# Raw output weights in the down-weight pool's five buffers, kept open through the output projection's first half

## The chip, the cores and the metric

The kernel runs on one NeuronCore of a Trainium2 chip. The metric is device time in microseconds (us) of one execution; the kernel before is shown by the median of three runs. TensorE (PE in the profile, PEld for its weight loads), VectorE (DVE), ScalarE (ACT) and GpSimd (POOL) compute, each with its own instruction stream in a fixed order; every DMA of this kernel is issued from SyncE's queue (SP), also in a fixed order, and runs on the core's 16 DMA engines.

## The reference

The program is one hybrid decoder layer on 1040 tokens (16 meta tokens and 1024 inputs) of width 1024, all in float32. Two head groups run in parallel on the same normalised input: four differential-attention heads and four HGRN2 heads (a gated linear recurrence in chunks of 16 tokens). Their outputs, 512 + 512 columns, are joined and multiplied by the output weights `w_out` (1024 x 1024); the result is normalised, added to the stream, and a gated FFN with a width-3 convolution follows.

```python
a = rmsnorm(h, ln_mix_pre[l])
dq, dk, dv, hq, hf, hi, hg = jnp.split(a @ w_in[l], SPLITS, axis=-1)
y_diff = diff_attention(dq, dk, dv, ...)          # 4 heads
y_hgrn = hgrn2(hq, hf, hi, hg, ...)               # 4 heads, recurrence over chunks
mix = jnp.concatenate([y_diff, y_hgrn], axis=-1) @ w_out[l]
h = h + rmsnorm(mix, ln_mix_post[l])
a = rmsnorm(h, ln_ffn_pre[l])
y = conv_ffn(a, w_ffn_up[l], ffn_conv_w[l], ffn_conv_b[l], w_ffn_down[l])
h = h + rmsnorm(y, ln_ffn_post[l])
```

The change concerns the product with `w_out`.

## The kernel before

Float32 products are made from three matmuls of rounded pieces: each operand is split into a high part (a cast by ACT) and a low part (raw minus high, by DVE or POOL), and high x high, high x low and low x high are summed in PSUM. So every weight tile goes through three steps: a DMA brings the raw 128 x 512 tile (256 KB), ACT casts the high part, and DVE or POOL subtracts for the low part.

The raw tiles pass through pools with a set number of buffers. A tile's DMA waits until the last reader of the buffer's former tile is done. The pool `wp` has three such raw buffers (tag `wr`). Another pool, `wsp` ("wdsums"), has five buffers of the same size (tag `wd`); it is used while the heads are computed, by `down_sums`: it loads quarters of the FFN's down weights (`wd11`, `wd12`, `wd21`, `wd22`), DVE subtracts them from each other, and the differences are written to the DRAM scratch `tsc`. Pools are stacked from the left or from the right end of the on-chip memory, and a pool that is closed gives its place to those opened after it. Before, `wsp` lay on the left, opened after the activations' pool and before the attention heads' pool `ap_`, and was closed with both when the last head's projections had been issued (line 923).

The output projection comes in two halves of 512 columns. `out_first` is the first half. It is issued interleaved with the last HGRN head (`hgrn_head`): its matmuls fill PE between that head's steps. Per block of 128 tokens (in the order 2, 3, 4, 5, 6, 7, 8, 1, then the meta tokens) it multiplies seven of the eight weight tiles k = 0 to 6 (the eighth belongs to the HGRN head that is not yet finished), in two parts, k = 0 to 3 and k = 4 to 6. The weights of this half are `wor0_k` (raw), `woh0_k` and `wol0_k` (high and low; for k = 0 and 1 they are called `wh`, `wl`). While it runs, the weights of the second half (`wor1_k`) are loaded and split, two or one per block. The tokens' own operand is split too: `mix_split` makes `mm`i`_0` (k = 0 to 3) and `mm`i`_4` (k = 4 to 6) of block i, with a cast on ACT and a subtraction on DVE, and writes them to the DRAM scratch `msc` by DMA for the second half, which loads them as `mp`.

The recurrence of the HGRN head runs in doubling steps on DVE and PE: DVE scales `mix` and `kr` (the keys), PE multiplies them into `pl`, DVE masks the result into `a` and `am`, and after the last step PE transposes `kr` into `pk` (line 518).

PE's order is written out by hand: the program order, set by `interleave`. On ACT, DVE, POOL and SP a scheduler orders instructions when the program is built, by its own costs and by the order of the code; `tc.issue_after` holds an instruction's place back behind another one. Most helpers on ACT and DVE have line 54.

Of the kernel before, what the change touches and what calls it, by code (L numbers as in the profile page):

```python
# [9 lines left out]
F32 = mybir.dt.float32  # L10
# [7 lines left out]
P = 128  # L18
# [4 lines left out]
KD = D // P  # L23
# [64 lines left out]
def layer_kernel(ctx: ExitStack, tc: tile.TileContext, x, meta, table, lbl, gpre, gpost, win,  # L88
# [6 lines left out]
    def pool(name, bufs, side="left", space=None):  # L95
        kw = {"side": side} if space is None else {"space": space}
        cm = tc.tile_pool(name=name, bufs=bufs, reuse_waits="tile", **kw)
        return cm, cm.__enter__()

    def line_up(where, n):  # L100
        where.tile([P, n], F32, tag=f"lineup{len(lined)}", name=f"lineup{len(lined)}", bufs=1)
        lined.append(n)
# [3 lines left out]
    def close(*cms):  # L106
        for cm in cms:
            cm.__exit__(None, None, None)
# [7 lines left out]
    w_cm, wp = pool("weights", 1, "right")  # L116
# [29 lines left out]
    def ps_in(name):  # L146
        return pp.tile([P, 512], F32, tag="ip", name=name)
# [4 lines left out]
    def ps_s(name):  # L152
        return pp.tile([P, 2, 512], F32, tag="S", name=name)

    def split(hi, lo, raw, eng=None):
        A.copy(hi, raw)
        (eng or G).tensor_tensor(lo, raw, hi.bitcast(F32), op=ALU.subtract)
# [18 lines left out]
    def mix(ks, t0, t1):  # L176
        g = 0 if t1 <= start(3) else 1 if t1 <= start(6) else 2
        base = start(GROUPS[g][0])
        return mixes[g][:, ks, t0 - base:t1 - base]

    at_cm, atp = pool("at", 1)
# [6 lines left out]
        base = start(GROUPS[g][0])  # L188
        return acts[l][g][:, ks, t0 - base:t1 - base]

    ws_cm, wsp = pool("wdsums", 5)
    wsp.tile([P, 32], F32, tag="lineup_ws", name="lineup_ws", bufs=1)

    last_load = []

    def down_sums():
        def load(k):
            with tc.issue_after(last_load[-1].ins):
                for nm, kk, half in (("11", k, 0), ("12", k, 1), ("22", k + NF // 2, 1), ("21", k + NF // 2, 0)):
                    b[nm] = wsp.tile([P, 512], F32, tag="wd", name=f"wd{nm}_{k}")  # L200
                    SY.dma_start(b[nm], wdown[P * kk: P * (kk + 1), 512 * half: 512 * (half + 1)])
            b["t3"] = wsp.tile([P, 512], F32, tag="wd", name=f"wd3_{k}")

        b = {}
        load(0)
        yield
        yield
        for k in range(NF // 2):
            for j, d, p_, q_ in ((2, "t3", "22", "12"), (0, "12", "12", "11"), (1, "22", "22", "12"), (3, "21", "21", "22")):
                with tc.issue_after(V.last.ins):  # L210
                    V.tensor_tensor(b[d], b[p_], b[q_], op=ALU.subtract)
                with tc.issue_after(last_load[-1].ins):
                    SY.dma_start(tsc[j][P * k: P * (k + 1)], b[d])
                yield
            if k + 1 < NF // 2:
                load(k + 1)
                yield
                yield
# [4 lines left out]

    wd_sums = down_sums()
    at_p_cm, ap_ = pool("attn", 1)
    z_cm, zp = pool("pre", 2, "right")

    def load_m(m, name, where=None, bufs=4):
# [143 lines left out]
    def carried():  # L372
        tails = list(carry)
        carry.clear()
        return tails
# [502 lines left out]
    for c in range(2):  # L878
        raw = wp.tile([P, 512], F32, tag="wr", name=f"wr3_{c}", bufs=3)
# [25 lines left out]
    h_cm, hp = pool("hgrn", 1, "right")  # L905
# [14 lines left out]

    assert next(wd_sums, wd_sums) is wd_sums
    line_up(hp, 24)
    close(at_p_cm, ws_cm, at_cm)
    y_cm, yp = pool("y0", 1)
    y0 = yp.tile([P, NBLK, 512], F32, tag="y0", name="y0")
    m0 = yp.tile([P, KD, 36], F32R, tag="m0", name="m0")
# [10 lines left out]
    ma_cm, map_ = pool("mixsplit", 4)  # L937
    w0_cm, w0p = pool("wo0", 1)
    line_up(w0p, 16)

    FIRST = (2, 3, 4, 5, 6, 7, 8, 1)
    kept = kpp.tile([P, 2, KD, P], F32R, tag="kept", name="kept")

    def load_wr(n, k):
        raw = wp.tile([P, 512], F32, tag="wr", name=f"wor{n}_{k}", bufs=3)
        last_load.append(SY.dma_start(raw, wout[P * k: P * (k + 1), 512 * n: 512 * (n + 1)]))
        return n, k, raw

    def load_wo(n, k, raw):
        if k < 2:  # L950
            where, tag, bufs = wp, ("wh", "wl"), 4
        elif n == 0 and k < KD - 1:
            where, tag, bufs = w0p, ("woh", "wol"), KD - 3
        else:
            where, tag, bufs = w1p, ("woh", "wol"), KD - 1
        hi, lo = (where.tile([P, 512], F32R, tag=t, name=f"{t}{n}_{k}", bufs=bufs) for t in tag)
        split(hi, lo, raw, V if n or k else G)
        return hi, lo

    def tok(i):  # L960
        return (2, 14) if i == 0 else (P, start(i))

    def mix_split(i, k0, k1):
        r, t0 = tok(i)
        src = mix(slice(k0, k1), t0, t0 + r)
        if i < 2:
            hi, lo = (kept[:, 0, k0:k1], kept[:, 1, k0:k1]) if i else (m0[:, k0:k1, 0:2], m0[:, k0:k1, 32:34])
        elif k1 - k0 == 1:
            m = mlp.tile([P, 2, 1, P], F32R, tag="m1", name=f"mm{i}_{k0}", bufs=7)
            hi, lo = m[:, 0], m[:, 1]  # L970
        else:
            m = map_.tile([P, 2, k1 - k0, P], F32R, tag="mm", name=f"mm{i}_{k0}")
            hi, lo = m[:, 0], m[:, 1]
        A.copy(hi, src)
        V.tensor_tensor(lo, src, hi.bitcast(F32), op=ALU.subtract)
        if i > 1 and k1 < KD:
            for c in range(k0 // 2, (k1 + 1) // 2):
                ka, kb = max(k0, 2 * c), min(k1, 2 * c + 2)
                SY.dma_start(msc[i, c][:, :, P * (ka - 2 * c):P * (kb - 2 * c)],
                             m[:, :, ka - k0:kb - k0].bitcast(F32).rearrange("p l k t -> p l (k t)"))  # L980
        return hi, lo, k0, k1, r

    def out_part(sp_, py, wo, first, last, ks=None):
        mh, ml, k0, k1, r = sp_
        for k in ks or range(k0, k1):
            hi, lo = wo[k]
            j = k - k0
            T.matmul(py[:r], mh[:, j, :r], hi, start=(first and j == 0), stop=False)
            yield 216
            T.matmul(py[:r], mh[:, j, :r], lo, start=False, stop=False)  # L990
            yield 216
            T.matmul(py[:r], ml[:, j, :r], hi, start=False, stop=(last and k == k1 - 1))
            yield 216
# [4 lines left out]
                T.matmul(py[:34], m0[:, k, :34], wo[k][l], start=(k == 0 and l == 0), stop=(k == last and l == 1))  # L998
                yield 216

    sps = [mix_split(i, 0, 4) for i in FIRST[:2]]
    mix_split(0, 0, 7)
    wo0 = [load_wo(*load_wr(0, k)) for k in range(KD)]
    wo = []

    pre_last = {}
# [19 lines left out]
    def mix_load(i, c):  # L1026
        m = mlp.tile([P, 2, 2, P], F32R, tag="mp", name=f"mp{i}_{c}", bufs=4)
        n = 1 if c == 3 else 2
        last_load.append(SY.dma_start(m[:, :, :n].bitcast(F32).rearrange("p l k t -> p l (k t)"), msc[i, c][:, :, : n * P]))
        return m[:, 0], m[:, 1], 2 * c, 2 * c + n, P  # L1030
# [3 lines left out]
    def out_first():  # L1034
        pys = [ps_s(f"py0_{i}")[:, 0] for i in FIRST[:2]]
        for ks in ((0, 1), (2, 3)):
            for j in range(2):
                yield from out_part(sps[j], pys[j], wo0, ks[0] == 0, False, ks)
        sqs = [mix_split(i, 4, 7) for i in FIRST[:2]]
        for j in range(2):  # L1040
            yield from out_part(sqs[j], pys[j], wo0, False, True)
            if j == 0:
                sp_ = mix_split(FIRST[2], 0, 4)
            A.copy(y0[:, FIRST[j]], pys[j])
        nxt = [load_wr(1, k) for k in (0, 1)]
        for n, i in enumerate(FIRST[2:]):
            for w in nxt:
                with tc.issue_after(V.last.ins):
                    wo.append(load_wo(*w))
            nxt = [load_wr(1, k) for k in ((2, 3), (4,), (5,), (6,), (7,), ())[n]]  # L1050
            if n == 3:
                ahead.extend(mix_load(2, c) for c in range(4))
            py = ps_in(f"py0_{i}")
            sq_ = mix_split(i, 4, 7)
            yield from out_part(sp_, py, wo0, True, False)
            if i != FIRST[-1]:
                sp_ = mix_split(FIRST[n + 3], 0, 4)
            yield from out_part(sq_, py, wo0, False, True)
            A.copy(y0[:, i], py)
        py = ps_in("py0_0")  # L1060
        yield from out_meta(py, wo0, 0, 7, 6)
        A.copy(y0[:2, 0], py[32:34])
        V.tensor_tensor(y0[:2, 0], y0[:2, 0], py[:2], op=ALU.add)
        while 0 not in finished:
            yield None
        for p in range(3):
            pre_last[p] = mix_split(p, 7, 8)
        for p in range(3):
            yield from out_last(p)

    interleave(out_first(), [hgrn_head(t_h, finished)] + carried(), FO, 4200)
    close(w0_cm, ma_cm, h_cm)

    sw_cm, swp = pool("sums", 1, "right")
    e_cm, ep = pool("early", 1, "right")
# [166 lines left out]
    for n, i in enumerate(order):  # L1242
# [9 lines left out]
        nxt = []  # L1252
# [507 lines left out]
```

## Time and profile before

| what | value |
|---|---|
| time, median of 3 runs | 1304.05 us (1303.45 to 1305.43) |
| the profiled execution, time | 1303.76 us |
| its span, first to last instruction | 1302.0 us |
| PE busy | 1270.9 us, 98% of the span |
| DVE, ACT, POOL busy | 913.7, 691.4, 408.7 us |
| granted TensorE clock | 0.999 |
| DMA | 153.07 MB, 118 GB/s on average |

The profiled execution took 1303.76 us, of which its span is 1302.0 us; the rest lies around it. The page's slices of the span show PE at nine tenths or more in all but the first and the last slice, at a full granted clock. The output projection's first half runs from about 518 us to 582 us of the span. In the rows of the timeline the columns are start and duration in us, engine, line, operation, result <- operands, size, count, and in brackets the idle time before it with what ended it.

### The profile page before, as it was taken

The page shows a single profiled execution, that of the slowest core. Times are in us where ns is not written, and L with a number is a line of the kernel's source. Part 1 is how long each engine was busy: PE and PEld are TensorE (multiplying, and loading weights), DVE is VectorE, ACT ScalarE, POOL GpSimd, SP SyncE. Part 2 cuts the span into 40 slices and gives each one's busy share as a digit, 9 for nine tenths or more (in the row PEclk, how much of TensorE's full clock was granted, in tenths as well). Part 3 has the DMA queues.
Part 4 walks back from the last instruction along what each step waited for, and adds up shares of the span by engine and source line. Part 5 has one row for each costly group of instructions (what it writes and reads, how often), then busy time and mean ns, then how long its engine had stood idle before and what let it go on. Part 6 is the DMA issues. An engine that isn't in the chain of part 4 may idle for free.

```text
span 1302.0 us, 26327 instructions
## 1 busy us (share of the span) xinstructions
PE 1270.9 (98%) x10236; PEld 1181.6 (91%) x10236; DVE 913.7 (70%) x1577; ACT 691.4 (53%) x1672; POOL 408.7 (31%) x322
## 2 busy tenths in 40 slices
PE   7999999999999999999999999999999999999997
PEld 6899999999998999777899999999999998888886
DVE  7575656575757565746888787787787787697587
ACT  7465356545653566446665454455455454454454
POOL 3211212021212120013155666766766740010020
PEclk9999999999999999999999999999999999999999
DMA  6221323122322211836711322222222236965363
GB/s 221 93 90 62 100 90 105 54 99 98 98 78 91 77 38 44 268 106 206 260 58 66 106 93 79 74 97 75 74 98 74 74 106 218 333 203 172 94 210 122
DMA packets 84371, 153.07 MB, mean 118 GB/s; under 512 B 9571, under 2 KB 19843, under 8 KB 84246
## 3 DMA queue, kind: packets, MB, share of 16 engines
q1 hardware_dynamic: 84246, 151.39, 35.2%
q8 instruction: 80, 1.31, 0.4%
q14 instruction: 45, 0.37, 0.1%
HBM read 112.69 MB, written 38.67 MB: 116 GB/s over the span
## 4 chain that ended last, share of the span: by engine, by line
PE 87%; DVE 6%; ACT 3%; DMA 2%; issue 1%; SPq 0%; DVEq 0%; ACTq 0%
PE pd L1571 5%; PE pd L1572 5%; PE pd L1570 5%; PE pb L1371 4%; PE pb L1372 4%; PE pb L1373 4%; PE pa L722 3%; PE pa L1372 3%; PE pa L1371 3%; PE pa L1373 3%; PE pc L1371 3%; PE pc L1373 3%; PE pc L1372 3%; PE pq L1350 2%; PE pq L1348 2%; PE pq L1349 2%
## 5 line engine op out<-in xcount | busy, mean ns | idle before, releaser
L1371 PE MATMUL pb<-t,uh 128*128 128x258 f32 (+1 forms) x456 | 127.4, 279 | 0.4 <-DVE u L54 0.4
L1372 PE MATMUL pb<-t,uh 128*128 128x258 f32 (+1 forms) x456 | 127.3, 279 | 0.0
L1373 PE MATMUL pb<-t,ul 128*128 128x258 f32 (+1 forms) x456 | 127.2, 279 | 0.0
L1571 PE MATMUL pd<-wl,gh 128*128 128x512 f32 (+1 forms) x314 | 120.8, 385 | 0.4 <-DVE wl L54 0.3
L1572 PE MATMUL pd<-wh,gl 128*128 128x512 f32 (+1 forms) x314 | 120.8, 385 | 0.0
L1570 PE MATMUL pd<-wh,gh 128*128 128x512 f32 (+1 forms) x314 | 120.7, 384 | 0.0
L54 DVE SCALAR_TENSOR_TENSOR c<-uu,cwt,c 128x512 f32<-128x512 f32 x88 | 94.7, 1077 | 22.3 <-ACT c L54 21.5
L1320 POOL TENSOR_TENSOR c<-c,c 128x512 f32<-128x512 f32 x44 | 64.4, 1463 | 127.2 <-ACT c L54 113.7
L54 DVE SCALAR_TENSOR_TENSOR c<-ug,cwt,c 128x512 f32<-128x512 f32 x88 | 84.0, 955 | 6.6 <-ACT c L54 5.9
L1371 PEld LDWEIGHTS pb<-t,uh 128*128 128x128 f32 x456 | 85.9, 188 | 0.8 <-DVE u L54 0.6
L1372 PEld LDWEIGHTS pb<-t,uh 128*128 128x128 f32 x456 | 85.9, 188 | 0.0
L1373 PEld LDWEIGHTS pb<-t,ul 128*128 128x128 f32 x456 | 85.8, 188 | 0.0
L1372 PE MATMUL pa<-t,uh 128*128 128x256 f32 (+1 forms) x304 | 85.3, 281 | 0.0
L1373 PE MATMUL pa<-t,ul 128*128 128x256 f32 (+1 forms) x304 | 85.2, 280 | 0.0
L1371 PE MATMUL pa<-t,uh 128*128 128x256 f32 (+1 forms) x304 | 85.2, 280 | 0.0
L1373 PE MATMUL pc<-t,ul 128*128 128x256 f32 x304 | 83.9, 276 | 0.0
L1371 PE MATMUL pc<-t,uh 128*128 128x256 f32 x304 | 83.9, 276 | 0.0
L1372 PE MATMUL pc<-t,uh 128*128 128x256 f32 x304 | 83.9, 276 | 0.0
L1571 PEld LDWEIGHTS pd<-wl,gh 128*128 128x128 f32 x314 | 59.0, 188 | 13.7 <-DVE wl L54 1.5
L1572 PEld LDWEIGHTS pd<-wh,gl 128*128 128x128 f32 x314 | 59.0, 188 | 12.0
L1570 PEld LDWEIGHTS pd<-wh,gh 128*128 128x128 f32 x314 | 59.0, 188 | 11.9
L54 ACT ACTIVATE c<-ug,cbt,cwt 128x512 f32<-128x512 f32 x44 | 35.9, 816 | 44.1 <-issue 26.2
(411 smaller groups left out, 4285.7 us busy)
## 6 DMA issues: line engine op xcount, KB each, us to landing
ra<-in_wup_dram SPq DMA_DIRECT2D x76, 256.0 KB, 2.7
wd<-in_wdown_dram SPq DMA_DIRECT2D x44, 256.0 KB, 3.3
tsc<-wd SPq DMA_DIRECT2D x44, 256.0 KB, 2.1
gsc<-c SPq DMA_DIRECT2D x44, 256.0 KB, 2.0
wi<-tsc SPq DMA_DIRECT2D x44, 256.0 KB, 3.0
gi<-gsc SPq DMA_DIRECT2D x33, 256.0 KB, 3.8
wi<-in_wdown_dram SPq DMA_DIRECT2D x33, 256.0 KB, 3.3
msc<-mm SPq DMA_DIRECT2D x21, 256.0 KB, 4.6
```

The lines of the kernel that those rows point to most:

```text
L54: ins = call(*args, **kw)
L722: T.matmul(po[:, :P], w_, vn[:, j], start=(j == 0), stop=(j == i))
L1320: G.tensor_tensor(cg, cg, cu, op=ALU.mult)
L1348: T.matmul(pt, hi[:, s], th[:, k], start=(kh + k == 0), stop=False)
L1349: T.matmul(pt, hi[:, s], tl[:, k], start=False, stop=False)
L1350: T.matmul(pt, lo[:, s], th[:, k], start=False, stop=(kh == 1 and k == 3))
L1371: T.matmul(pt, hi[:, s], th[:, k], start=(first and k == 0), stop=False, skip_group_check=True)
L1372: T.matmul(pt, hi[:, s], tl[:, k], start=False, stop=False, skip_group_check=True)
L1373: T.matmul(pt, lo[:, s], th[:, k], start=False, stop=(k == 3), skip_group_check=True)
L1570: T.matmul(py, gh[:, s], wh, start=(k == 0 and pr not in (3, 7)), stop=False, skip_group_check=True)
L1571: T.matmul(py, gh[:, s], wl, start=False, stop=False, skip_group_check=True)
L1572: T.matmul(py, gl[:, s], wh, start=False, stop=(k == NH - 1), skip_group_check=True)
```

## The change

The pool `wsp` moves from the left to the right end of the memory, so that it lies next to `wp`, and it is no longer closed before the output projection but after its first half, together with the HGRN pool. `load_wr` now puts only the first three raw tiles of the first half (k = 0, 1, 2) into `wp`'s three buffers; all others go into the five buffers of `wsp`, which `down_sums` has done with by then. All eight loads of the first half are written ahead of the first `mix_split`s, and of the second half's loads four instead of two are written ahead of the block loop, which then keeps more loads ahead of the splits. Small pads (`line_up`) are moved with the pools. The pools of the attention and HGRN heads thereby lie 10,240 bytes lower in each partition; what is opened after the first half lies where it did.

```diff
-    ws_cm, wsp = pool("wdsums", 5)
-    wsp.tile([P, 32], F32, tag="lineup_ws", name="lineup_ws", bufs=1)
+    ws_cm, wsp = pool("wdsums", 5, "right")
...
     wd_sums = down_sums()
     at_p_cm, ap_ = pool("attn", 1)
+    line_up(ap_, 32)
...
-    close(at_p_cm, ws_cm, at_cm)
+    close(at_p_cm, at_cm)
...
     def load_wr(n, k):
-        raw = wp.tile([P, 512], F32, tag="wr", name=f"wor{n}_{k}", bufs=3)
+        raw = (wp.tile([P, 512], F32, tag="wr", name=f"wor{n}_{k}", bufs=3) if n == 0 and k < 3
+               else wsp.tile([P, 512], F32, tag="wd", name=f"wor{n}_{k}"))
         last_load.append(SY.dma_start(raw, wout[P * k: P * (k + 1), 512 * n: 512 * (n + 1)]))
         return n, k, raw
...
-    sps = [mix_split(i, 0, 4) for i in FIRST[:2]]
+    wors = [load_wr(0, k) for k in range(KD)]
+    with tc.issue_after(last_load[-1].ins):
+        sps = [mix_split(i, 0, 4) for i in FIRST[:2]]
     mix_split(0, 0, 7)
-    wo0 = [load_wo(*load_wr(0, k)) for k in range(KD)]
+    wo0 = [load_wo(*w) for w in wors]
...
-        nxt = [load_wr(1, k) for k in (0, 1)]
+        nxt = [load_wr(1, k) for k in range(4)]
         for n, i in enumerate(FIRST[2:]):
-            for w in nxt:
+            for w in [nxt.pop(0) for _ in range((2, 2, 1, 1, 1, 1)[n])]:
                 with tc.issue_after(V.last.ins):
                     wo.append(load_wo(*w))
-            nxt = [load_wr(1, k) for k in ((2, 3), (4,), (5,), (6,), (7,), ())[n]]
+            nxt += [load_wr(1, k) for k in ((4,), (5,), (6,), (7,), (), ())[n]]
...
-    close(w0_cm, ma_cm, h_cm)
+    close(w0_cm, ma_cm, h_cm, ws_cm)
```

PE's and POOL's orders stay as they were. On SP, before the output projection, where the last loads of the input weights (`wr_hg3`) and the last writes of the differences (`tsc`) stand, the rows were, before:

```order
L213 DMA tsc_93<-wd3_10_5284 128x512
L163 DMA wr_hi3_1_5698<-in_win_dram 128x512
L163 DMA wr_hg3_0_5887<-in_win_dram 128x512
L213 DMA tsc_93<-wd12_10_5278 128x512
L213 DMA tsc_93<-wd22_10_5280 128x512
L213 DMA tsc_93<-wd21_10_5282 128x512
L163 DMA wr_hg3_1_5893<-in_win_dram 128x512
L946 DMA wor0_0_6343<-in_wout_dram 128x512
L946 DMA wor0_1_6349<-in_wout_dram 128x512
L946 DMA wor0_2_6355<-in_wout_dram 128x512
L946 DMA wor0_3_6361<-in_wout_dram 128x512
L946 DMA wor0_4_6367<-in_wout_dram 128x512
```

and are now:

```order
L212 DMA tsc_93<-wd3_10_5284 128x512
L947 DMA wor0_3_6336<-in_wout_dram 128x512
L163 DMA wr_hi3_1_5698<-in_win_dram 128x512
L163 DMA wr_hg3_0_5887<-in_win_dram 128x512
L212 DMA tsc_93<-wd12_10_5278 128x512
L947 DMA wor0_4_6338<-in_wout_dram 128x512
L212 DMA tsc_93<-wd22_10_5280 128x512
L947 DMA wor0_5_6340<-in_wout_dram 128x512
L212 DMA tsc_93<-wd21_10_5282 128x512
L947 DMA wor0_6_6342<-in_wout_dram 128x512
L947 DMA wor0_7_6344<-in_wout_dram 128x512
L163 DMA wr_hg3_1_5893<-in_win_dram 128x512
```

The five loads that take over buffers of the differences stand each behind the write that frees its buffer, and ahead of the last input weight; the three that stay in `wp` follow after it. The loads `wor0_5` to `wor0_7` stood much later before, behind the first writes to `msc`.

On ACT, at the start of the first half, the rows were, before (`sg` is the HGRN head's gate, `m0` and `kept` the splits of the meta tokens and of block 1):

```order
L54 CAST mm2_4_6461<-mix0_99 128x384
L54 ACTIVATE sg3_2_6292<-pi_hg3_2_6250 128x384
L54 CAST m0_6306<-mix0_99 128x7x2
L54 CAST mm3_4_6466<-mix1_100 128x384
L54 CAST kept_6330<-mix0_99 128x512
L54 ACTIVATE sg3_2_6292<-sg3_2_6292,one_80 128x384
L54 CAST kept_6330<-mix0_99 128x384
L54 ACTIVATE sg3_2_6292<-sg3_2_6292 128x384
L54 CAST mm4_0_6485<-mix1_100 128x512
L54 CAST woh0_5_6375<-wor0_5_6373 128x512
L54 CAST woh0_6_6381<-wor0_6_6379 128x512
L54 CAST woh0_7_6387<-wor0_7_6385 128x512
```

and are now:

```order
L54 CAST woh0_5_6378<-wor0_5_6340 128x512
L54 ACTIVATE sg3_2_6292<-pi_hg3_2_6250 128x384
L54 CAST m0_6305<-mix0_99 128x7x2
L54 CAST woh0_6_6382<-wor0_6_6342 128x512
L54 CAST woh0_7_6386<-wor0_7_6344 128x512
L54 ACTIVATE sg3_2_6292<-sg3_2_6292,one_80 128x384
L54 CAST mm2_4_6460<-mix0_99 128x384
L54 ACTIVATE sg3_2_6292<-sg3_2_6292 128x384
L54 CAST mm3_4_6465<-mix1_100 128x384
L54 CAST kept_6329<-mix0_99 128x512
L54 CAST mm4_0_6484<-mix1_100 128x512
L54 CAST wh1_0_6548<-wor1_0_6540 128x512
```

The casts of `woh0_5` to `woh0_7` come ahead of the tokens' splits, and the place behind `mm4_0` is taken by `wh1_0`, the first weight of the second half.

On ACT, near the end of the first half (`am` are copies for the HGRN head's masked products), the rows were, before:

```order
L54 CAST mm7_0_6847<-mix2_101 128x512
L54 CAST woh1_5_6862<-wor1_5_6804 128x512
L54 COPY y0_6305<-py0_5_6685 128x512
L54 CAST mm7_4_6877<-mix2_101 128x384
L54 CAST woh1_6_6929<-wor1_6_6866 128x512
L54 COPY am_736<-a323_6415 32x8x32 x4
L54 CAST mm8_0_6908<-mix2_101 128x512
L54 CAST woh1_7_7010<-wor1_7_6933 128x512
L54 COPY y0_6305<-py0_6_6806 128x512
L54 CAST mm8_4_6936<-mix2_101 128x384
```

and are now:

```order
L54 CAST mm7_0_6848<-mix2_101 128x512
L54 CAST woh1_7_7009<-wor1_7_6867 128x512
L54 COPY y0_6304<-py0_5_6686 128x512
L54 CAST mm7_4_6878<-mix2_101 128x384
L54 COPY am_736<-a323_6414 32x8x32 x4
L54 CAST mm8_0_6909<-mix2_101 128x512
L54 COPY y0_6304<-py0_6_6807 128x512
L54 CAST mm8_4_6935<-mix2_101 128x384
```

`woh1_7`, the last weight, moves up by one block, to where `woh1_5` stood, and no weight's cast stands between `mm7_4` and `mm8_4` any more.

## The prediction

> **What bounds the kernel now.** I read the engines' shares first, then the busy time by stretch, then what PE waited for, and then the timeline of PE, ACT, DVE and SP at each wait. First the page's engine rows, then the stretches of the span (per engine: us busy, instructions in brackets; then PE clock, DMA share, GB/s):
>
> ```profile
> PE 1270.9 (98%) x10236; PEld 1181.6 (91%) x10236; DVE 913.7 (70%) x1577; ACT 691.4 (53%) x1672; POOL 408.7 (31%) x322
> ...
> 525.00:532.00 7.00, 5.35 (x85) 3.41 (x84) 5.12 (x12) 4.47 (x8) 0.00 (x0) 1.00 0.96 328
> 532.00:555.00 23.00, 23.00 (x386) 17.88 (x386) 18.27 (x48) 9.59 (x19) 2.34 (x5) 1.00 0.82 250
> 555.00:560.00 5.00, 3.18 (x16) 2.33 (x15) 2.38 (x5) 1.99 (x4) 0.00 (x0) 1.00 0.34 115
> ```
>
> PE is the bound: a change is worth what it opens or closes in PE's stream. The first half of the output projection has two holes, 7.00 - 5.35 = 1.65 us of idle time before 532 and 5.00 - 3.18 = 1.82 us before 560; between them PE is full. What each waited for, from PE's and ACT's timelines:
>
> ```profile
> 524.88 0.39 PE L990 MATMUL py<-wol,mm 128*128 128x512 f32 x1
> 525.11 0.39 PE L992 MATMUL py<-woh,mm 128*128 128x512 f32 x1
> 526.64 0.51 PE L988 MATMUL py<-woh,mm 128*128 128x512 f32 x1 [1.15 <-ACT woh L54]
> ...
> 528.67 0.49 PE L580 MATMUL ssa<-ident,ona 128*128 128x128 f32 x3
> ...
> 530.36 0.69 PE L462 MATMUL pl<-mix,kr 128*32 128x16 f32 x62 [0.28 <-DVE am L54]
> ...
> 534.00 0.70 PE L462 MATMUL pl<-mix,kr 128*32 128x16 f32 x62
> ...
> 555.94 0.40 PE L992 MATMUL py<-woh,mm 128*128 128x512 f32 x1
> 558.16 0.55 PE L518 MATMUL pk<-ident,kr 128*128 128x128 f32 x3 [1.82 <-DVE kr L54]
> ```
>
> ```profile
> 522.55 0.62 ACT L54 CAST mm<-mix 128x512 fp32r<-128x512 f32 x1 [1.17 <-PE py L992]
> 525.97 1.93 ACT L54 CAST woh<-wor 128x512 fp32r<-128x512 f32 x3 [2.80 <-DMA wor<-in_wout_dram]
> ...
> 545.41 0.62 ACT L54 CAST woh<-wor 128x512 fp32r<-128x512 f32 x1 [1.86 <-DMA wor<-in_wout_dram]
> ...
> 555.13 0.62 ACT L54 CAST woh<-wor 128x512 fp32r<-128x512 f32 x1 [3.44 <-DMA wor<-in_wout_dram]
> 556.13 0.51 ACT L54 CAST mm<-mix 128x384 fp32r<-128x384 f32 x1
> ```
>
> Both begin with a raw output weight that has not landed. At 525.97 ACT has stood 2.80 us before `woh0_5`, which PE needs next. At 555.13 it has stood 3.44 us before `woh1_7`, which nobody needs yet; but the cast of `mm8_4` is queued behind it, and behind that, on DVE, `kr`:
>
> ```profile
> 526.62 0.69 DVE L54 TENSOR_TENSOR wol<-wor,woh 128x512 fp32r<-128x512 f32 x1 [2.73 <-ACT woh L54]
> ...
> 530.94 0.36 DVE L54 TENSOR_TENSOR mix<-mix,f 128x192 f32<-128x192 f32 x1 [0.26 <-PE pl L462]
> 531.21 0.69 DVE L54 TENSOR_TENSOR mm<-mix,mm 128x512 fp32r<-128x512 f32 x1
> 531.82 0.69 DVE L54 TENSOR_TENSOR kr<-kr,f 128x520 f32<-128x520 f32 x1
> 532.43 0.56 DVE L54 TENSOR_TENSOR mix<-mix,f 128x136 f32<-128x136 f32 x2
> ...
> 552.93 0.28 DVE L54 TENSOR_TENSOR mix<-mix,tt 128x128 f32<-128x128 f32 x1
> 556.67 0.56 DVE L54 TENSOR_TENSOR mm<-mix,mm 128x384 fp32r<-128x384 f32 x1 [3.46 <-ACT mm L54]
> ...
> 557.42 0.69 DVE L54 TENSOR_TENSOR kr<-kr,tt 128x512 f32<-128x512 f32 x1
> ```
>
> Why the weights are late stands in SP's queue and in the time from issue to landing of the eleven `wor` loads after 515 us:
>
> ```profile
> 446.68 8.18 SPq L213 DMA_DIRECT2D tsc<-wd  x3
> 460.04 0.33 SPq L163 DMA_DIRECT2D wr_hg<-in_win_dram  x1
> 461.29 40.06 SPq L946 DMA_DIRECT2D wor<-in_wout_dram  x5
> ...
> 519.81 1.53 SPq L946 DMA_DIRECT2D wor<-in_wout_dram  x3
> ...
> 548.30 0.56 SPq L946 DMA_DIRECT2D wor<-in_wout_dram  x1
> ...
> 566.36 12.37 SPq L1231 DMA_DIRECT2D rap<-in_wup_dram  x4
> DMA to landing us min/median/max: 2.9/4.7/6.8
> ```
>
> With three buffers only five loads are out before 502; `wor0_5` is issued at 519.81, when an earlier split has freed a buffer, and lands 6.2 us later, at 525.97.
>
> **The first hole.** The five extra loads now go out behind the writes of the differences (446.68 to 454.86), and `wor0_0` to `wor0_2` take the three old buffers. All eight land by about 482, since the last old buffer is freed by the split of the second `wr_hg`, whose cast comes at 476.2 (row below). ACT then casts `woh0_5` to `woh0_7` before 521, with no wait. Without it PE runs on from 525.11: nine matmuls of three weight steps at 0.23 us (524.88 to 525.11), plus some 0.3 us for the HGRN head's three `ssa` transposes between them (528.67), bring the next `pl` to 525.11 + 10 x 0.23 + 0.3 = 527.75 instead of 530.36. That is 2.6 us; the idle time of 1.65 is its lower bound, as the restarts at 0.50 us are also paid.
>
> A part is lost to ACT's new order. `wh1_0` now stands behind `mm4_0`, and its load is issued where `wor0_5` was and should land as late, at 526. So ACT still stands from 523.2 to 526, takes three weight casts (1.93 us) and only then `mm4_4`; PE needs that one late, but DVE's subtraction for it stands before the doubling step. By the rows that is 528.4 for the cast's end, then on DVE about 0.5 each for `mm4_4` and `kept`, as their shape is that of 556.67, and 0.3, 0.6, 0.6 and 0.5 for the four rows from 530.94 on, by the distance of their starts: 531.4 to 531.8. PE would be at its second `pl` at 527.75 + (534.00 - 530.36) = 531.4. I take 0.35 us off, bounds 0 and 1.0 (one load a us later). First term: 2.25 us, bounds 1.3 and 2.6.
>
> **The second hole.** `wor1_7` went out at 548.30, when the split of `wor1_4` had freed a buffer. With five buffers it gets that of `wor1_2`, split two blocks earlier, and goes out about 538, in SP's order behind two `mp` loads. Its cast moves to the place where `woh1_5` stood, and no weight stands between `mm7_4` and `mm8_4`. It should land at 543, by the median of 4.7 us, when ACT arrives at 541 (545.41 - 1.86 in the row of `woh1_5`, less the first term); `woh1_5` cost 1.86 us there and PE stayed full (23.00 of 23.00). Then `mm8_4` is cast as soon as its block is done, DVE goes from 552.93 straight to `mm`, `mix` and `kr` (some 1.6 us by the rows from 556.67 to the end of `kr`: done by 554.7), and PE finds `kr` ready at 555.94 + 0.23 = 556.17 instead of 558.16. Second term: 2.0 us. Its lower bound is 0, if `wor1_7` takes 6.8 us and stalls DVE's chain at the new place by as much.
>
> **Moved and added at no cost.** The casts and subtractions are as many as before (16 weights, 0.62 us on ACT and 0.69 on DVE by the rows of 555.13 and 526.62), only in another order. SP gains waits: `wor0_3`, `wor0_5`, `wor0_6` and `wor0_7` wait until the difference in their buffer has been written out, and behind them stands `wr_hg3_1`, issued at 460.04. These writes land within 2.1 us:
>
> ```profile
> tsc<-wd SPq DMA_DIRECT2D x4, 256.0 KB, 2.0
> ...
> L54 ACT CAST wh_hg<-wr_hg x2: 620/620/621, 472.9 to 476.2; 128x512 fp32r<-128x512 f32 x2
> ```
>
> That ends near 457, before the buffer of `wr_hg3_1` is free, and its cast comes at 476.2, so 13 us of cover lie behind that. Should the writes take longer than this, ACT and then PE's gate projection would wait for the rest. After 582 the orders are the old ones and follow PE. The sum is 2.25 + 2.0 = 4.25 us, less 0.1 for the small things: the span of 1302.0 becomes 1297.9, the profiled run's 1303.76 becomes 1299.6, and the median of the runs, 0.29 above that run, 1299.9 us.
>
> The Trainium skill, "SBUF — State Buffer", section "The DMA setup-cost knee", gives a transfer some 2 us fixed plus its bytes at 436 GB/s: an estimate of 2.6 us for 256 KB by that page. By it `wor0_5` would have landed at 522.4, before ACT was free at 523.2, and the first term would be nothing. The trace does not agree where it counts: 6.2 us here, a median of 4.7, with the DMA engines at 0.96 between 525 and 532.
>
> **Rivals.** (a) One hole stays or comes back elsewhere. Either `wor1_7` lands late at its new place, or `wh1_0` and its followers hold ACT longer in the first stretch. For it speaks that the loads out after 519 are as many and the engines at 0.96; against it that the loads come earlier than their use by a block. It leaves one term: 1304.05 - 2.1 = 1302.0. (b) The change doesn't do what it says: the stand merely moves from `woh0_5` to `wh1_0` and on to what PE needs. For it: the same landing time, 526. Against it: behind `wh1_0` PE first needs `mm4_4`, five us later. Time: 1303.5 to 1304.5. (c) Slower, through SP after the first half: `rap0_11`, the first FFN weight, was issued at 566.36 into the place of `kr`. With the HGRN pool 10 KB lower its place is that of `on`, the normalised HGRN output, which PE reads last in the `ss` transposes at 576.87; all SP rows behind it, the loads of `gpo` and `xh` among them, wait too, and on ACT its cast stands at 580.72. Its rows, the landing of the four `rap` loads, and a later wait of PE:
>
> ```profile
> 576.87 0.55 PE L580 MATMUL ss<-ident,on 128*128 128x128 f32 x3
> ...
> 580.72 1.73 ACT L54 CAST uh<-rap 128x512 fp32r<-128x512 f32 x3
> ...
> 588.87 0.60 ACT L54 ACTIVATE at<-py 128x512 f32<-128x512 f32 x1 [3.21 <-PE py L992]
> ...
> DMA to landing us min/median/max: 2.6/2.8/4.0
> ...
> PE py L988 <- DMA mp<-msc: 0.8, 1, 0.8
> ```
>
> Before, the second `rap` load waited for that same read, so the queue only gets one issue (0.4 us) later, and a landing in 2.6 to 4.0 us puts the cast at most 1 us late, against 3.21 us that ACT idles next. It decides from 3.2 us on; to make the kernel 0.2% slower it would have to be 4.1 + 2.6 + 3.2, some 10 us late: 1307. On this queue the Trainium skill, "DMA: Bandwidth & Descriptors", section "Anatomy of one DMA", says that a semaphore wait happens on the issuing sequencer and not in the DMA engines; by it, (c) has a queue behind it, as I have taken it.
>
> **Numbers.** 0.2% is 2.6 us, about what a measurement of this kernel can tell from no change. Forecast (both holes close): 0.70, 1298.7 to 1301.3. (a) 0.15 and (b) 0.10, both within 0.2% for the most part. (c) and other losses 0.05. Faster 0.71, same 0.24, slower 0.05. The range runs from 1298.6 (2.6 + 2.0 and the 0.8 us that PE waits for `mp` later, should that wait go too) to 1302.6, past (a), with (b) and (c) left out.
>
> **What would show it.** In the profile of the changed kernel: ACT's `woh0_5` cast before 520 with no wait; no PE wait for `woh` or `wol` near 525; the `pk` transposes within 0.3 us of the matmul before them; `wor1_7` issued before 541. A PE wait on `pl` for `mix` or `am` between 529 and 536 would be the lost part of the first term. I am wrong if PE waits there for more than a us, if ACT stands at `woh1_7` beyond 545, or if PE's waits after 600 grow beyond the 0.8 us for `mp`.

## The result, and the profile after

The changed kernel takes 1299.62 us, median of 8 runs (1299.01 to 1300.77); the kernel before 1303.43 us, median of 8 (1301.70 to 1305.43). The medians differ by 3.8 us. The ratio on record is 0.9974, with a 95% interval of 0.9964 to 0.9985, so 0.26% or 3.4 us faster (2.0 to 4.7). A second series of 11 runs beside other kernels gave 1300.33 us against 1303.57, ratio 0.9979 (0.9971 to 0.9988). The profiled execution after took 1299.51 us, its span is 1297.7 us, so 4.3 us less than the profiled span before, as the working had it (4.1).

The page's engine rows and the stretches of the span after, with the same columns as before:

```profile
PE 1269.4 (98%) x10236; PEld 1180.8 (91%) x10236; DVE 913.6 (70%) x1577; ACT 691.9 (53%) x1672; POOL 410.3 (32%) x322
...
525.00:532.00 7.00, 7.00 (x158) 5.42 (x156) 4.78 (x13) 6.09 (x12) 0.00 (x0) 1.00 1.03 351
532.00:555.00 23.00, 23.00 (x337) 18.04 (x330) 18.70 (x48) 8.71 (x18) 2.49 (x5) 1.00 0.70 229
555.00:560.00 5.00, 5.00 (x30) 4.32 (x29) 0.99 (x3) 1.07 (x2) 0.00 (x0) 1.00 0.01 2
```

PE is full in all three stretches: the 1.65 and the 1.82 us of idle time are gone. PE's timeline after:

```profile
525.00 0.39 PE L993 MATMUL py<-woh,mm 128*128 128x512 f32 x1
525.22 0.39 PE L989 MATMUL py<-woh,mm 128*128 128x512 f32 x1
...
527.73 0.71 PE L462 MATMUL pl<-mix,kr 128*32 128x16 f32 x62
...
531.36 0.74 PE L462 MATMUL pl<-mix,kr 128*32 128x16 f32 x62
...
553.31 0.39 PE L993 MATMUL py<-woh,mm 128*128 128x512 f32 x1
553.55 0.49 PE L518 MATMUL pk<-ident,kr 128*128 128x128 f32 x3
```

The matmul behind the one at 525.00 starts 0.22 us later where it stood 1.15 us before; `pl` comes at 527.73 (before: 530.36), and the `pk` transposes at 553.55 (before: 558.16), 0.24 us behind the matmul ahead of them. On ACT:

```profile
516.45 2.17 ACT L54 CAST woh<-wor 128x512 fp32r<-128x512 f32 x4
...
525.44 0.62 ACT L54 CAST wh<-wor 128x512 fp32r<-128x512 f32 x1 [2.37 <-DMA wor<-in_wout_dram]
...
544.45 0.62 ACT L54 CAST woh<-wor 128x512 fp32r<-128x512 f32 x1 [3.48 <-DMA wor<-in_wout_dram]
```

`woh0_5` is the last of the four casts from 516.45 on, with no wait. ACT still stands 2.37 us, now before `wh1_0`, and 3.48 us before `woh1_7`, but PE did not wait for what is queued behind them in this execution. After 560 us the longest of PE's waits are these:

```profile
PE py L989 <- DMA mp<-msc: 0.7, 1, 0.7
PE pz L989 <- DVE y L54: 0.7, 1, 0.7
PE pb L1374 <- DVE u L54: 0.6, 1, 0.6
```

### The profile page after: what moved, and what is told of

The parts are those of the page before. It is cut to its first block, busy times and chain, and to the rows that moved or that the text cites. A ratio compares the mean times of both kernels' runs of the same rounds, so it can differ in the third digit from the quotient of the medians.

```text
span 1297.7 us, 26321 instructions
## 1 busy us (share of the span) xinstructions
PE 1269.4 (98%) x10236; PEld 1180.8 (91%) x10236; DVE 913.6 (70%) x1577; ACT 691.9 (53%) x1672; POOL 410.3 (32%) x322
## 4 chain that ended last, share of the span: by engine, by line
PE 87%; DVE 7%; ACT 2%; DMA 2%; issue 1%; SPq 0%; POOL 0%; DVEq 0%; ACTq 0%; POOLq 0%
PE pd L1574 5%; PE pd L1575 5%; PE pd L1573 4%; PE pb L1374 4%; PE pb L1375 4%; PE pb L1376 4%; PE pa L722 3%; PE pa L1375 3%; PE pa L1374 3%; PE pa L1376 3%; PE pc L1376 3%; PE pc L1374 3%; PE pc L1375 3%; PE pq L1353 2%; PE pq L1351 2%; PE py L989 2%
## 5 line engine op out<-in xcount | busy, mean ns | idle before, releaser
L1198 POOL TENSOR_TENSOR ws<-ra,ra 128x512 f32<-128x512 f32 x38 | 56.9, 1498 | 8.5 <-DMA ra<-in_wup_dram 5.7
```

The source lines that it names most:

```text
L1198: G.tensor_tensor(sums[nm], a, b, op=op)
```

## The experiments

The kernels were timed in four series, each with its own runs of the kernel before: its medians were 1303.40 us (the first four rows after "after" in the table, 35 runs of the kernel before), 1303.57 (the next four), 1302.78 (the next three) and 1302.91 (the last).

| kernel | median, us | ratio, 95% interval | wait for `woh`, us | first `pk`, us | wait for `mp`, us |
|---|---|---|---|---|---|
| before | 1303.43 | | 1.1 | 558.16 | 0.8 |
| after | 1299.62 | 0.9974, 0.9964 to 0.9985 | 0 | 553.55 | 0.7 |
| pools_only | 1302.79 | 0.9998, 0.9990 to 1.0007 | 0.2 | 554.96 | 0.5 |
| first_half | 1300.25 | 0.9980, 0.9971 to 0.9989 | 0 | 554.34 | 0.6 |
| second_half | 1302.09 | 0.9992, 0.9984 to 1.0001 | 0.6 | 555.25 | 0.6 |
| cast_later | 1302.61 | 0.9997, 0.9989 to 1.0006 | 1.4 | 557.43 | 0.9 |
| fewer_writes | 1300.74 | 0.9981, 0.9972 to 0.9990 | 0.6 | 556.12 | 1.2 |
| first_half_cast_later | 1300.20 | 0.9982, 0.9974 to 0.9991 | 0 | 553.71 | 0.4 |
| after_safe | 1299.57 | 0.9974, 0.9966 to 0.9983 | 0 | 553.40 | 0.5 |
| after_again (the changed kernel) | 1300.33 | 0.9979, 0.9971 to 0.9988 | 0 | 554.73 | 1.0 |
| gpo_later | 1300.43 | 0.9975, 0.9964 to 0.9986 | 0 | 554.08 | 0.9 |
| three_buffers_safe | 1300.27 | 0.9975, 0.9964 to 0.9987 | 0 | 554.40 | 2.9 |
| after_safe_gpo | 1299.88 | 0.9975, 0.9963 to 0.9987 | 0 | 553.76 | 0.6 |
| gpo_rows | 1301.66 | 0.9992, 0.9983 to 1.0001 | 0.4 | 556.39 | 2.0 |

The last three columns are PE's waits and the start of the first `pk` transposes in the one profiled execution of each kernel. They are not averages, and the first experiment shows how far one execution can lie from the median. Differences in us are those of the medians unless the text says that they are by the ratio. The last series ran on another chip than the three ahead of it, so its kernel is compared with its own runs of the kernel before.

### The pools alone

```diff
-    ws_cm, wsp = pool("wdsums", 5)
+    ws_cm, wsp = pool("wdsums", 5, "right")
...
-    close(w0_cm, ma_cm, h_cm)
+    close(w0_cm, ma_cm, h_cm, ws_cm)
```

> The pools lie as in the changed kernel (the five buffers at the right end and open through the first half, the heads' pools 10,240 bytes lower), but all raw output weights still go through the three old buffers, written and issued as before. Theory (the gain is two holes closed by raw weights that land earlier): as before, within 0.5 us of 1303.4; PE's waits for woh (1.1 us) near 525 and for kr (1.8 us) near 556 stand as they did. Rival (the places in memory or the later close make the gain): about 1299.6, with both waits gone.

1302.79 us, ratio 0.9998: no difference that can be told. Where the pools lie and when they close earns at most 1.3 us (0.9990), not the whole change. But the profiled execution was one of its fastest, 1300.35 us, and the second hole was not in it. PE, ACT and SP there:

```profile
525.51 0.49 PE L988 MATMUL py<-woh,mm 128*128 128x512 f32 x1 [0.22 <-ACT woh L54]
...
554.96 0.49 PE L518 MATMUL pk<-ident,kr 128*128 128x128 f32 x3
```

```profile
549.65 0.62 ACT L54 CAST woh<-wor 128x512 fp32r<-128x512 f32 x1 [0.39 <-DMA wor<-in_wout_dram]
```

```profile
546.45 0.34 SPq L946 DMA_DIRECT2D wor<-in_wout_dram  x1
```

With the loads of before, `wor1_7` landed here 549.65 - 546.45 = 3.2 us after its issue, not 6.8, and PE did not wait for `kr` at all; the first hole was 0.22 us rather than 1.15. The holes that the old loads make are no fixed sum: they differ with the landing times. That may be why the 35 runs of the kernel before spread from 1301.23 to 1304.88 us; only one of its executions was profiled, so the runs do not show it.

### One half at a time

The changed kernel with the condition of `load_wr` altered, and the old loop of the second half; in its counterpart the condition is `n == 0`, and the loads of the first half are written as before.

```diff
-        raw = (wp.tile([P, 512], F32, tag="wr", name=f"wor{n}_{k}", bufs=3) if n == 0 and k < 3
+        raw = (wp.tile([P, 512], F32, tag="wr", name=f"wor{n}_{k}", bufs=3) if n == 1 or k < 3
                else wsp.tile([P, 512], F32, tag="wd", name=f"wor{n}_{k}"))
```

> Only the first half's raw weights go to the five buffers, early; the second half's go through the three old buffers in the old order of code. Theory: the first hole closes and the second stays: 2.5 us less than before, 1300.9; no PE wait for woh near 525, PE waits 1.8 us for kr before the pk transposes. Rival (one hole only shifts the other, since the later one takes up what the first gives): 1303.0 to 1304 or 1299.5.

> Only the second half's raw weights go to the five buffers, early; the first half's go through the three old buffers in the old order of code. Theory: the second hole closes and the first stays: 2.0 us less than before, 1301.4; PE waits 1.1 us for woh near 525 and not for kr. With the kernel that changes the first half alone the sum should be the whole gain, 3.8 to 4.5 us, if the holes are independent.

The first half alone gives 3.15 us (1303.40 - 1300.25), by the ratio 2.6 (1.4 to 3.8), so it can't be told from the 2.5 expected nor from the whole change; the second alone 1.3, with an interval from no change to 2.1, which just takes in the 2.0 expected. Together they would be 4.5, against 3.8 and 3.2 measured for the whole change. With intervals of more than a us on each side this neither shows nor refutes that the holes are independent. PE, ACT and SP in the kernel with the first half alone:

```profile
527.75 0.70 PE L462 MATMUL pl<-mix,kr 128*32 128x16 f32 x62
...
532.17 0.70 PE L462 MATMUL pl<-mix,kr 128*32 128x16 f32 x62 [0.69 <-DVE mix L54]
...
554.34 0.49 PE L518 MATMUL pk<-ident,kr 128*128 128x128 f32 x3
```

```profile
526.70 0.62 ACT L54 CAST woh<-wor 128x512 fp32r<-128x512 f32 x1 [3.07 <-DMA wor<-in_wout_dram]
...
548.44 0.62 ACT L54 CAST woh<-wor 128x512 fp32r<-128x512 f32 x1 [0.88 <-DMA wor<-in_wout_dram]
```

```profile
545.83 0.33 SPq L947 DMA_DIRECT2D wor<-in_wout_dram  x1
```

The second hole is not there although its weights go through the three old buffers: `wor1_7` landed in 2.6 us. Six raw weights are loaded between 515 and 560 us here, eleven before; the other five went out before 515 us. The relief of the queue is a candidate for why the second hole is rarer, though one execution does not prove it, since the old loads can land as fast. The wait of 0.69 us at the second `pl` is the loss that the prediction took off the first term: ACT stands at a second-half weight (`woh1_2` here) until 526.70 and `mm4_4` is late.

### The second hole without buffers

```diff
         A.copy(hi, src)
+        casts[i, k0] = A.last
...
-                with tc.issue_after(V.last.ins):
+                with tc.issue_after(V.last.ins), tc.issue_after((casts[8, 4] if w[1] == 7 else V.last).ins):
                     wo.append(load_wo(*w))
```

> The kernel before, with its three buffers and its late load of wor1_7, but ACT casts woh1_7 behind the cast of mm8_4 instead of ahead of it. Theory (the second hole is ACT's queue: kr is late only because mm8_4's cast stands behind a weight that has not landed): the hole closes without any buffer, 2.0 us less than before, 1301.4, and ACT stands at woh1_7 with nobody waiting. Rival (the late landing itself, or the DMA engines' load, holds the chain): the wait for kr stays at 1.8 us and the time at 1303.4.

1302.61 us, ratio 0.9997: not told from no change, so the expected 2.0 us is not there. In its profile PE does not wait for `kr`. But ACT now stands at the weight before, and the chain is almost as late:

```profile
551.69 0.62 ACT L54 CAST woh<-wor 128x512 fp32r<-128x512 f32 x1 [3.65 <-DMA wor<-in_wout_dram]
...
555.30 0.62 ACT L54 CAST woh<-wor 128x512 fp32r<-128x512 f32 x1
```

```profile
554.54 0.69 DVE L54 TENSOR_TENSOR mm<-mix,mm 128x512 fp32r<-128x512 f32 x1 [2.13 <-ACT mm L54]
...
556.69 0.68 DVE L54 TENSOR_TENSOR kr<-kr,tt 128x512 f32<-128x512 f32 x1
```

`woh1_6` stood 3.65 us, `mm8_0` and the DVE rows behind it were late, and `kr` was done at 557.37 (556.69 + 0.68), just before `pk` at 557.43. PE came there 1.2 us later than in the profile of before (its first `pl` stands at 531.59, not at 530.36, after a wait of 1.4 us for `woh`), so the wait is gone in this execution with nothing to spare. The mechanism, a cast queued behind a weight that has not landed, is shown twice over; that moving one cast buys the whole hole is refuted.

The same edit in the kernel that changes the first half alone:

> The kernel that changes the first half alone, and in it ACT's cast of woh1_7 behind that of mm8_4. Theory: what the second half's buffers give beyond the first half's, 0.6 us by the medians so far, is the stand at woh1_7 in those executions in which it lands late; with the cast out of the way the kernel comes to 1299.7, as the whole change. Rival (the early loads of the second half do something else, in the stretch after 560 us or on the queue): it stays at 1300.3. Against both works ACT's stand at woh1_2, which made PE wait 0.7 us for mix at the second pl in the kernel that changes the first half alone: it should be there again.

1300.20 us, the same as the first half alone (1300.25) and as the changed kernel in the same series (1300.33). The stand at `woh1_2` was there (2.06 us), the wait at the second `pl` was not in this execution. That is 0.5 us above the 1299.7 that was expected and where the rival had it. So nothing is left for the second half's buffers that these runs could measure: once the first half's loads are early, the kernel is as fast without them.

### Every second-half cast out of the way

```diff
             sq_ = mix_split(i, 4, 7)
+            for w in now:
+                with tc.issue_after(casts[i, 4].ins), tc.issue_after(V.last.ins):
+                    wo.append(load_wo(*w))
```

> The changed kernel, but every split of a second-half weight stands behind ACT's cast of the block's second mix part (wh1_0 and wh1_1 behind mm4_4, and so on to woh1_6 behind mm8_4). Theory: no weight of the second half can then hold a chain that PE waits for, so the stand of 2.4 us at wh1_0 and that of 3.5 us at woh1_7 go; as PE did not wait for either in the profile of the changed kernel, the profile stays at 1297.5 to 1297.8 us of span, and the median goes down only by what other executions lose there, 0 to 0.5 us: 1299.1 to 1299.6. Rival (such stands cost nothing in any execution): 1299.6. It would be slower only if the later splits were late for the second half, which begins at about 582.

> The changed kernel once more, on the same chip as the three others, for an interval beside theirs. Theory: 1299.6, 3.8 us less than before, and between its fastest and slowest executions under 2 us where the kernel before has 3.7.

1299.57 us, from 1298.96 to 1300.24 over 11 runs; the unaltered change in the same series 1300.33, from 1299.35 to 1301.46, so 0.7 us above what was expected of it and with a spread of 2.1 us. ACT no longer stands at any raw weight of the second half (`wh1_0` at 525.75 and `woh1_7` at 549.76 start with no wait). The means, 1299.61 and 1300.36, differ by 0.75 us with a standard error of 0.25 (standard deviations of 0.40 and 0.74). The first series of the changed kernel, beside other runs of the kernel before, had 1299.62, so I take this as a version that is better by 0 to 0.8 us. Its runs lie closer together here, but two more kernels with late casts, at the end of the next section, spread from 1299.25 to 1302.41 and from 1299.39 to 1301.79; that late casts make a kernel steadier is not shown. One loss that they take away is in the second profile of the plain change, an execution of 1300.80 us:

```profile
531.89 0.70 PE L462 MATMUL pl<-mix,kr 128*32 128x16 f32 x62 [0.29 <-DVE mix L54]
```

Here the loss at the second `pl` that the first profile did not show is present: 0.29 us. It is a small part of the 1.3 us by which this execution is the longer one.

### What the raw weights stand behind

The weight that makes the first hole takes 6.2 us to land. The next kernel writes only one of the four `msc` pieces per block and reads that one back for all four, so that most writes between 502 and 560 us fall away.

```diff
-            for c in range(k0 // 2, (k1 + 1) // 2):
+            for c in range(k0 // 2, 1):
...
-        last_load.append(SY.dma_start(m[:, :, :n].bitcast(F32).rearrange("p l k t -> p l (k t)"), msc[i, c][:, :, : n * P]))
+        last_load.append(SY.dma_start(m[:, :, :n].bitcast(F32).rearrange("p l k t -> p l (k t)"), msc[i, 0][:, :, : n * P]))
```

> The kernel before, with three buffers and late loads, but of the four DRAM pieces per block that hold the split tokens for the second half only the first is written, and the second half reads that one in the place of all four (so its result is wrong). Most of the msc writes between 502 and 560 us fall away. Theory now (a raw weight issued late lands late because it stands behind those writes, and by how much differs between executions: 6.2 us for wor0_5 and 6.8 for wor1_7 in the profile of before, 5.2 at most in the kernel with the pools alone): wor0_5 and wor1_7 land in about 3 us, ACT does not make PE wait for woh0_5, kr is not late, and the time is 1299.6 to 1300.6 without a single new buffer. Rival (a landing of 5 to 7 us is what such a load takes, or the late issue alone decides): landings stay above 4.5 us and the time at 1303.4.

1300.74 us, 2.8 us less, with three buffers, and just above the stretch expected. The median landing of the weights after 515 us fell from 4.7 to 2.7 us. Yet one load was as slow as ever; the landings and ACT:

```profile
DMA to landing us min/median/max: 2.4/2.7/6.9
```

```profile
521.43 0.61 ACT L54 CAST woh<-wor 128x512 fp32r<-128x512 f32 x1
...
526.25 0.62 ACT L54 CAST woh<-wor 128x512 fp32r<-128x512 f32 x1 [4.20 <-DMA wor<-in_wout_dram]
```

`wor0_5`, issued at 518.53 ahead of the load of `gpo0`, was there at 521.43 with no wait. `wor0_6`, issued at 519.47 right behind it, landed at 526.25, and PE waited 0.6 us for it. So I looked at the DMA rate around `gpo0`, the gain of the output norm: one DRAM row of 2 KB, read 128 times. Its issue and the stretches of the kernel before (last two columns: share of the DMA engines' time, GB/s):

```profile
518.53 0.62 SPq L931 DMA_DIRECT2D gpo<-in_gpost_dram  x1
```

```profile
518.00:520.00 2.00, 2.00 (x10) 1.69 (x10) 2.00 (x6) 2.00 (x7) 0.00 (x0) 1.00 1.09 369
520.00:522.00 2.00, 2.00 (x10) 1.61 (x10) 2.00 (x5) 1.39 (x4) 0.00 (x0) 1.00 0.47 111
522.00:524.00 2.00, 2.00 (x73) 1.46 (x72) 1.09 (x2) 0.62 (x1) 0.00 (x0) 1.00 0.84 268
524.00:526.00 2.00, 1.50 (x7) 0.89 (x5) 0.00 (x0) 0.03 (x1) 0.00 (x0) 1.00 1.07 389
```

Behind that load, issued at 518.53, the sixteen engines move 111 GB/s where they move 369 and 389 around it. `wor0_5` was issued at 519.81. The other profiles agree: in the nine whose queue has the load at this place, that of before among them, the rate from 520 to 522 us is 82 to 144 GB/s. Two kernels test it: one issues the load of `gpo0` after the last `msc` write, the other leaves it where it is but fills `gpo0` with 128 different rows of the output weights.

```diff
-    SY.dma_start(gpo0, gpost[:, :512].to_broadcast([P, 512]))
...
+        with tc.issue_after(last_msc[-1].ins):
+            SY.dma_start(gpo0, gpost[:, :512].to_broadcast([P, 512]))
```

```diff
-    SY.dma_start(gpo0, gpost[:, :512].to_broadcast([P, 512]))
+    SY.dma_start(gpo0, wout[:P, :512])
```

> The kernel before, with its three buffers, but the load of gpo0 (one DRAM row of 2 KB read 128 times, first needed by POOL after 577 us) is issued after the last msc write, about 553, instead of just ahead of wor0_5. In the profile of before the DMA engines move 111 GB/s from 520 to 522 us behind that load and 389 from 524 to 526. Theory (the row read again and again slows all sixteen engines for some 2.5 us, and wor0_5 stands behind it): wor0_5 lands by 523.5, ACT's stand before woh0_5 is under 0.5 us, the first hole closes and with it 2.3 to 3.0 us: 1300.4 to 1301.2, the second hole left as it is. Rival (the slow stretch is that of the msc writes or of the queue's start, the broadcast only stands there): landing of wor0_5 stays at 5 to 6 us, 1303.4.

> The kernel before, order for order, but gpo0 is filled with 128 different DRAM rows (the first 128 rows of the output weights, 512 columns, the same 256 KB) instead of one row read 128 times; its result is wrong by that gain. Theory (it is the one row read again and again that slows the engines): the rate from 520 to 522 us stays near 380 GB/s instead of 111, wor0_5 lands some 2 us earlier, by 524, and the time is 1300.6 to 1301.6, nearly that of the load moved away. Rival (256 KB more in the queue just there, whatever they are, delay wor0_5): the landing stays at 5 to 6 us and the time at 1303.4.

Moving that one load, with three buffers and no other edit, gives 1300.43 us, ratio 0.9975 (0.9964 to 0.9986). By the medians that is 2.3 us (1302.78 - 1300.43), as the theory had it, by the ratio 3.3: the larger part of the whole change, and by the ratio not told from it. Its stretch, the issue of `wor0_5` and its cast:

```profile
520.00:522.00 2.00, 2.00 (x11) 1.61 (x10) 2.00 (x5) 1.24 (x3) 0.00 (x0) 1.00 0.95 290
```

```profile
519.13 1.57 SPq L945 DMA_DIRECT2D wor<-in_wout_dram  x3
```

```profile
523.34 0.62 ACT L54 CAST woh<-wor 128x512 fp32r<-128x512 f32 x1 [2.10 <-DMA wor<-in_wout_dram]
```

`wor0_5` lands at 523.34, 4.2 us after its issue at 519.13, and PE waits for no `woh`. With 128 different rows in the old place the rate falls less, but the time is only 1301.66 us, ratio 0.9992 (0.9983 to 1.0001): just above the stretch expected, and by the ratio not told from no change. All is about 1.0 us later in its profiled execution, so the stretch that answers to 520 to 522 is 521 to 523; that stretch, the cast, and SP:

```profile
521.00:523.00 2.00, 2.00 (x11) 1.61 (x10) 2.00 (x5) 1.43 (x4) 0.00 (x0) 1.00 0.89 232
```

```profile
526.27 1.93 ACT L54 CAST woh<-wor 128x512 fp32r<-128x512 f32 x3 [2.06 <-DMA wor<-in_wout_dram]
```

```profile
520.85 1.63 SPq L946 DMA_DIRECT2D wor<-in_wout_dram  x3
```

`wor0_5` takes 5.4 us. So of 6.2 us, 2.0 go when the load is moved away, and 0.8 when it stays but reads many rows. The other profiles give the scatter: with the one-row load ahead of it `wor0_5` took 5.2 us in pools_only, 5.5 in second_half and 6.3 in cast_later, and with the load moved 4.3 in three_buffers_safe. The 4.2 lies outside that scatter, the 5.4 inside it and where the rival had it (5 to 6). That the one row lowers the rate is shown (232 GB/s with many rows, 82 to 144 with one); that this delays the weight more than any 256 KB ahead of it would is not shown.

The last two put both edits together, the late load of `gpo0` and the second-half splits behind the cast of their block: one in the kernel before, one in the changed kernel.

> The same with three buffers and gpo0 late, and every split of a second-half weight behind ACT's cast of the block's second mix part. Theory: both holes close without a new buffer, 1299.4 to 1300.0, with the narrow spread of the kernel that has the casts late and the five buffers (1299.0 to 1300.2). Rival (three buffers still let a split come too late for something, the loads' issue being held by the buffers): 1301 or more, with ACT's stands before woh0_5 or at the start of the second half.

> The changed kernel with the casts late, and gpo0 late too. Theory: there is no hole left between 505 and 560 us for it to close: 1299.3 to 1299.7, the same as without. Rival (the slow stretch costs the changed kernel something as well): 1298.8 or less; and slower, 1300 or more, if gpo0 just ahead of the rap loads makes ACT and PE wait for the first FFN weights after 580.

Without any new buffer: 1300.27 us, 0.3 us above the expected stretch and not told from the changed kernel. The narrow spread that was expected is not there. Between 505 and 560 us its PE waits 0.6 us in all, for `am`; the profiled execution, 1302.41 us, lost its time elsewhere:

```profile
PE py L992 <- DMA mp<-msc: 2.9, 3, 1.6
```

That is the second half's operand, in the crowded stretch from 600 to 640 us, which none of these edits touches. With everything together 1299.88 us, 0.2 us above the expected stretch and, as expected, no gain over 1299.57.

## Why the prediction was right, and where it was not

1. **The bound and the two places.** Right. PE lost its time where raw weights were late on ACT, and the profile after has no wait for `woh`, `wol` or `kr`. The pools alone give nothing that can be told, so the gain is that of the loads.
2. **First term, 2.25 us (1.3 to 2.6).** In the pair of profiles it is 530.36 - 527.73 = 2.6 us, 2.5 without the 0.11 us by which PE was already ahead at 525. The next `pl` was forecast at 527.75 and came at 527.73. The 0.35 us taken off for the second `pl` were 0 in the first profile, 0.29 in the second and 0.69 in the kernel with the first half alone: a loss that comes in some executions, of the size assumed.
3. **Second term, 2.0 us (0 to 2.0).** In the pair of profiles it is there: 4.61 us at `pk`, of which 2.6 were won before; of these 4.61 the span keeps 4.3, the rest is lost again in small waits later. Over the runs it is the term that was mis-sized. The step that failed is reading its size from one execution: with the old loads `wor1_7` landed in 6.8 us in the profile of before and in 3.2 in that of the pools alone, and at 3.2 there is no hole. Six profiled kernels keep the three buffers and the old order of casts for the second half (before, pools_only, first_half, fewer_writes, gpo_later, gpo_rows); PE waits for `kr` in that of before alone (the last three kernels also thin out or reorder what stands ahead in the queue). The second half alone is worth 1.3 us with an interval from 0 to 2.1, and beyond the first half's buffers nothing measurable. The sum of 4.25 us was 3.8 in one series and 3.2 in the other, by the ratios 3.4 and 2.7. So it is luck that the pair of profiles meets the sum to 0.2 us: it needed an execution of before with the second hole in full.
4. **The landing of `wor1_7`.** Forecast: out about 538, landed at 543. The row of its issue stands below: 539.92, and it landed at 544.45, 4.5 us, near the median of 4.7. That is 0.55 us short of the 545 from which I would have been wrong, and in the second profile 0.24 (the cast began at 544.76), so the margin was thin. Another sign of being wrong, a wait for `mp` beyond 0.8 us, did come in the second profile, with 1.0; in the table this wait ranges from 0.4 to 2.9 us, so that sign can't tell the change from one execution to the next.
5. **SP's extra waits at no cost.** Right: `wr_hg3_1`, behind the writes of the differences and the added loads, went out at 459.94, before at 460.04.

```profile
459.94 0.33 SPq L163 DMA_DIRECT2D wr_hg<-in_win_dram  x1
...
539.92 0.33 SPq L947 DMA_DIRECT2D wor<-in_wout_dram  x1
...
572.82 1.89 SPq L1234 DMA_DIRECT2D rap<-in_wup_dram  x4
```

6. **Rival (c), the late `rap`.** Its mechanism took place: the load went out at 572.82, before at 566.36, as its place is now that of `on`. ACT waited 1.5 us for it, where 1 us at most was forecast, as one of the four landed in 4.9 us rather than 4.0. PE shows no wait for it: ACT had 3.2 us to spare behind it before, and 1.7 after. (a) and (b) did not happen, though (b)'s picture did: ACT stands before `wh1_0` until 525.44, and it costs 0 to 0.3 us.
7. **What the prediction did not see.** It took the landing time of 6.2 us as given. The trace of before had a cause of it in the row of `gpo0` on SP at 518.53 and in the DMA rate behind it. Moving that one load earns about the first hole with no buffer.

On the rule of the Trainium skill, "SBUF — State Buffer", section "The DMA setup-cost knee", that was weighed: on a nearly idle queue (47 GB/s on average between 430 and 515 us) the trace agrees. The raw weights that the changed kernel issues between 430 and 515 us land in

```profile
DMA to landing us min/median/max: 2.4/2.8/3.1
```

against an estimate of 2.6 us by that page. With many transfers ahead in the queue it does not: after 515 us the median is 4.5 us in the same execution, 5.6 in its second profile, and a load took up to 6.8 before. Here the rule gives what a load costs alone, not when it lands.

## What to carry to other kernels

When an engine stands at a load, ask first what is ahead of that load in its queue; here one broadcast load that nobody needed for more than 50 us sat in front of the critical weight, and moving it was worth the larger part of what five more buffers gave. Keep an in-order engine's waits for late data behind the work that the bound needs next, so that a late landing costs less. And take the size of a hole that a DMA makes from several executions, since one profile shows one draw.

## What was not expected of the hardware

A load of 256 KB that reads one DRAM row of 2 KB 128 times took the rate of the sixteen DMA engines from 369 to 111 GB/s for about 2 us in the kernel before, at an engine share of 0.47; in the changed kernel it was 104 and 82 GB/s in two profiles, at engine shares of 0.93 and 0.87. The same 256 KB from 128 rows left 232. Why the rate falls is open. The same 256 KB load of a weight lands in 2.4 us on a nearly idle queue and in 7.4 at worst with many transfers ahead (`wor1_6` in the kernel with one cast moved). With the same loads in the same order, `wor1_7` took 6.8 us in the kernel before and 3.2 in that with the pools alone.
